# A decoder trunk in split fp32r products: inverse roots by one ScalarE function, LayerNorm sums by fp32r products, four more warm products, and the first sums moved into the third product group

## The chip, the core and the metric

The kernel runs on one core of a Trainium2 chip. The metric is device time in microseconds (us). The program is one launch over one step of a decoder trunk: 288 tokens (256 of a new sequence and 8 times 4 of running ones), width 2048, one layer, MLP width 8192.

## What is computed

```python
def trunk_layer(x, hist_conv, hist_pool, pos0, ...):
    h = rmsnorm(x, norm1_g)                              # x * rsqrt(mean(x*x) + EPS) * g
    proj = einsum("btd,de->bte", h, w_in) + b_in         # 2048 -> 1024 + 1024 + 1024
    a, gate, z = proj[..., :1024], proj[..., 1024:2048], proj[..., 2048:]
    u = a * sigmoid(gate)
    u_ext = concatenate([hist_conv, u], axis=1)          # 30 tokens of history
    c = silu(layernorm(depthwise_causal_conv(u_ext, conv_w, conv_b), ln_g, ln_b))   # 31 taps
    z_ext = concatenate([hist_pool, z], axis=1)          # 15 tokens of history
    d = multiscale_pool(z_ext, pos0)                     # windows 2, 4, 8, 16: mean - z
    p = einsum("btgc,gce->btge", d, pool_w) * pool_scale # four groups of 256
    x = x + einsum("btm,md->btd", concatenate([c, p]), w_out)
    f = square(relu(einsum("btd,df->btf", rmsnorm(x, norm2_g), w_ff1)))
    x = x + einsum("btf,fd->btd", f, w_ff2)
    return x, u_ext[:, -30:], z_ext[:, -15:]
# then y = rmsnorm(x, norm_f); both token sets share all weights
```

## The kernel before

Channels lie on the 128 partitions and the 288 tokens along the free axis. Every weight block and every activation is split into two fp32r parts, hi (a rounded copy) and lo (the rest), and each product of a 128x128 weight tile with 128x288 activations is three TensorE (PE) matmuls: hi by hi, lo by hi, hi by lo. All of them are recorded at line L305, in `mm`. The weights come once from memory by DMA on SP's queue into the tile `wr` (six buffers). The hi part `whi` is a cast on ScalarE (ACT), L274; the lo part `wlo` is a subtraction on VectorE (DVE), L279, or in two halves on GpSimd (POOL), L282, or a DMA that accumulates, L277. The string table `WAYS` says which block goes which way. Both parts have five buffers each, so a new cast has to wait until PE has read the block five before it.

The order of the program is: nine warm products (L213, L214) on a constant; sixteen blocks of `x` with their weights, split by `first_split` (L364 to L376); then one product group after another as the tuple `SEQUENCE` lists them: `c0` to `c7` are pairs of columns for the convolution branch (`c0` and `c1` run as one group of 384 products, `c2` is the second group, with 192), `p3` to `p0` are the input columns of the pool branch (`pool_group`), `P3` to `P0` its own small products (`pool_products`, tile `pp`). Then come eight product groups of `w_out` on the pool branch (right-hand side `dx`), eight on the convolution branch (`mx`), and four rounds of the MLP.

The first RMSNorm is not applied before the products but after them. `squares()` adds up x*x on ACT and DVE. `first_sums` (L524) sums over partitions by three small matmuls into PSUM tile `pt`, and `rsqrt_sums` turns the 96x3 sums into inverse roots: a DVE step (L249), a square root on ACT (L250), the load of the next ACT function table (L209), then four DVE steps (L253 to L256, one of them a reciprocal, one Newton step). `first_rows` (L528) spreads them over the partitions by three fp32 matmuls (`spread`), and ACT copies the result to the row `rb` (L530). A dictionary `between` says ahead of which pair of blocks of a group PE does this: the sums ahead of the last pair of the first group, the spread ahead of the second pair of `c2`. `conv_pair` and `pool_group` multiply their products by `rb` (L445, L483).

The convolution is 31 taps per pair of columns, each a DVE instruction of 128x256 (L461). `conv_pair` puts them under `later()`, a lower priority, so that the scheduler fills DVE with them between the steps that PE waits for. For the samples POOL makes all products at once (`prd`, L464) and DVE adds them (L466). In `pool_group` the scaled input `tz` (L483) becomes `z_all`; POOL adds windows (L492), mends the first columns (`rcnt`, L496), DVE makes the difference `d` (L497), POOL that of the samples (L499, L500), and `d` is split into `dx` hi (ACT, L502) and lo (DVE, L503). `pool_products` reads the product tile `pp` and writes `dx` again (L514, L515).

LayerNorm: `ln_mean` sums 1024 channels by two fp32 products with a matrix of ones (tile `pmean`); `ln_sums` centres, squares (L566) and adds (L570, L571) and calls `rsqrt_sums`; `ln_rows` spreads; the loop behind (L592 to L598) scales, applies Silu, and splits the result into `mx`. The second RMSNorm (`second_rows`) and the final one take the square root on ACT and call `inverse_root`, a DVE reciprocal (L233) and three more DVE steps. PSUM tiles made by `ms` (`warm`, `pt`, `pp`, `pmean`, `ends`) all use one single buffer.

Each engine runs its instructions in the order in which the scheduler put them, and an instruction that waits holds up all behind it on its engine.

Of the kernel before, what the change touches and what calls it, by code (L numbers as in the profile page):

```python
# [16 lines left out]
P = 128  # L17
D = 2048
# [68 lines left out]
def trunk_kernel(ctx: ExitStack, tc: tile.TileContext, io):  # L87
# [18 lines left out]
    def nm(s):  # L106
        seen[s] = seen.get(s, 0) + 1
        return f"{s}{seen[s]}"
# [25 lines left out]
    def f32(t):  # L134
        return t.bitcast(F32)
# [20 lines left out]
    def v(key, j):  # L156
        return vec[:, OFF[key] + j : OFF[key] + j + 1]
# [48 lines left out]

    def load_table(func, src):

        return nc.scalar.activation(few[: src.shape[0], :], src, func)  # L209

    load_table(AF.Sqrt, ones[:, 0:1])
    warm = ms("warm")
    for j in range(9):  # L213
        nc.tensor.matmul(warm[:, 0, 0:P], ones, ones, start=True, stop=True)  # L214
    ident = const.tile([TB, TB], F32, name="ident", padded_shape=[TB, TB + 40])
    make_identity(nc, ident)
# [9 lines left out]
    cst = const.tile([P, 32], F32, name="cst")  # L226
    eps, mean_d = cst[:, 0:1], cst[:, 1:2]
    nc.vector.memset(eps, EPS)
    nc.vector.memset(mean_d, 1.0 / D)

    def inverse_root(mean, root, y, out):

        nc.vector.reciprocal(y, root)  # L233
        nc.vector.scalar_tensor_tensor(out=root, in0=mean, scalar=EPS, in1=y, op0=ALU.add, op1=ALU.mult)
        nc.vector.scalar_tensor_tensor(out=root, in0=root, scalar=-0.5, in1=y, op0=ALU.mult, op1=ALU.mult)
        nc.vector.scalar_tensor_tensor(out=out, in0=root, scalar=1.5, in1=y, op0=ALU.add, op1=ALU.mult)

    def rsqrt_sums(parts, scale, after=None):

        pq = ms("pt")
        pt = pq[:, 0, :]
        for n, t in enumerate(parts):
            for j in range(3):
                last = mm(pt[:TB, j : j + 1], t[:, j * TB : (j + 1) * TB], ones[:, 0:1], start=n + j == 0, stop=n == len(parts) - 1 and j == 2)
        st = const.tile([TB, 12], F32, name=nm("st"))
        s = [st[:, 3 * j : 3 * j + 3] for j in range(4)]
        nc.vector.tensor_scalar(s[0], pt[:TB, 0:3], scale * DC, EPS, op0=ALU.mult, op1=ALU.add)  # L249
        nc.scalar.activation(s[1], s[0], AF.Sqrt)  # L250
# [3 lines left out]
        nc.vector.tensor_tensor(s[3], s[2], s[2], op=ALU.mult)  # L254
        nc.vector.scalar_tensor_tensor(out=s[3], in0=s[3], scalar=-0.5, in1=s[0], op0=ALU.mult, op1=ALU.mult)
        nc.vector.scalar_tensor_tensor(out=s[2], in0=s[3], scalar=1.5, in1=s[2], op0=ALU.add, op1=ALU.mult)  # L256
# [45 lines left out]
    def mm(*args, **kw):  # L302

        with tc.issue_after(chain[-1]) if chain else nullcontext():
            last = nc.tensor.matmul(*args, **kw)  # L305
        if chain:
            chain[0] = last.ins
        return last
# [50 lines left out]
    def first_split(k0):  # L359
        firsts.append([by_pair(t) for t in spl()])  # L360
        raw, hi, lo = raws[k0 // 2], *firsts[k0 // 2]
        blocks = [slice(i, i + 1) for i in range(2)] if k0 < 4 else [slice(0, 2)]
        hx.extend(halves(act2("hx")))
        nc.scalar.copy(hi[:, blocks[0]], raw[:, blocks[0]])  # L364
        for k in range(k0, k0 + 2):
            if k == 0:
                nc.vector.tensor_scalar(hx[k][0], xT[:, k, :], v("norm1_g", k), None, op0=ALU.mult)  # L367
            else:
                nc.scalar.activation(hx[k][0], xT[:, k, :], AF.Copy, scale=v("norm1_g", k))  # L369
        for b in blocks[1:]:  # L370
            nc.scalar.copy(hi[:, b], raw[:, b])
        for b in blocks:
            nc.vector.tensor_tensor(lo[:, b], raw[:, b], f32(hi[:, b]), op=ALU.subtract)
# [37 lines left out]
    def squares():  # L411

        nc.scalar.copy(scratch[:, :, :, 0:1], f32(firsts[2][0])[:, 1, 1, 0:10].rearrange("p (n k t) -> p n k t", n=5, t=1))
        for q in range(8):
            xq = xT[:, 2 * q : 2 * q + 2, :]
            a = q // 4
            dst = scratch[:, 2 + q % 3] if q % 4 else tot[a]
            nc.scalar.activation(dst, xq, AF.Square)
            if q % 4:
                nc.vector.tensor_tensor(tot[a], tot[a], dst, op=ALU.add)  # L420
        nc.vector.tensor_tensor(tot[0], tot[0], tot[1], op=ALU.add)
        nc.vector.tensor_tensor(tot[0][:, 0, :], tot[0][:, 0, :], tot[0][:, 1, :], op=ALU.add)
        return [tot[0][:, 0, :]]
# [98 lines left out]
    pair1 = [cvp.tile([P, 512], F32, name=nm("ac"), tag="cv") for m in range(2)]  # L522

    def first_sums():  # L524
        diag.append(rsqrt_sums(squares(), 1.0 / D, AF.Sigmoid))
        return diag[0][2]

    def first_rows():  # L528
# [10 lines left out]
    for kind, i in SEQUENCE[3:]:  # L539
# [5 lines left out]
            pool_group(i)  # L545
        else:
            pool_products(i)
    load_table(AF.Sqrt, f32(mixp[1][0])[:, 0:1])
# [4 lines left out]

    norm = {}

    def ln_mean():
        norm["mean"] = ms("pmean")[:, 0, :T]
        mm(norm["mean"], ones, sum_c[:, 0, :], start=True, stop=False)
        return mm(norm["mean"], ones, cs[-1][:, 1, :], start=False, stop=True)

    def ln_sums():
        ssc = None
        for c in cs:
            nc.vector.tensor_tensor(c, c, norm["mean"][:, None, :].to_broadcast([P, 2, T]), op=ALU.subtract)
            q = tmpp.tile([P, 2, T], F32, name=nm("q2"), tag="ag" if ssc is None else "ag2", bufs=2)
            nc.scalar.activation(q, c, AF.Square)  # L566
            if ssc is None:
                ssc = q
            else:
                nc.vector.tensor_tensor(ssc, ssc, q, op=ALU.add)  # L570
        nc.vector.tensor_tensor(ssc[:, 0, :], ssc[:, 0, :], ssc[:, 1, :], op=ALU.add)  # L571
        norm["sums"] = rsqrt_sums([ssc[:, 0, :]], 1.0 / DC, AF.Silu)
        return norm["sums"][2]

    def ln_rows():
        norm["rows"], last = spread(norm["sums"])
# [11 lines left out]

    mixc = []
    for j, c in enumerate(cs):  # L590
        n = tmpp.tile([P, 2, T], F32, name=nm("n"), tag="ag", bufs=2)
        nc.vector.tensor_tensor(n, c, norm["rows"][:, None, :].to_broadcast([P, 2, T]), op=ALU.mult)  # L592
        for m in range(2):
            i = 2 * j + m
            nc.scalar.activation(n[:, m, :], n[:, m, :], AF.Silu, bias=v("ln_b", i), scale=v("ln_g", i))  # L595
        mh, ml = act2("mx")
        nc.scalar.copy(mh, n)  # L597
        nc.vector.tensor_tensor(ml, n, f32(mh), op=ALU.subtract)  # L598
        mixc += halves((mh, ml))


# [36 lines left out]
    def second_rows():  # L638

        hl = actp.tile([P, 4, T], F32R, name="hl", tag="act")  # L640
        hi, lo = hl[:, 1, :], hl[:, 0, :]
        nc.scalar.copy(hi, ss2)
        nc.vector.tensor_tensor(lo, ss2, f32(hi), op=ALU.subtract)
        bk, r2 = ms("mean2"), row("r2")
        mean, root = bk[:, 0, :T], bk[:, 1, :T]
        mm(mean, means, hi, start=True, stop=False)
        last = mm(mean, means, lo, start=False, stop=True)
        nc.scalar.activation(root, mean, AF.Sqrt, bias=eps)
        inverse_root(mean, root, r2, r2)
        rows2.append(r2)  # L650
        return last

# [55 lines left out]
    nc.scalar.activation(root, sums_f, AF.Sqrt, bias=eps[:TB, :])  # L708
    inverse_root(sums_f, root, first, s_f)
    for spread_f in (rows_f, again):  # L710
        for j in range(3):
# [72 lines left out]
```

## Time and profile before

| what | value |
|---|---|
| time, median of three runs | 1084.62 us (1084.41 to 1085.51) |
| time of the profiled execution | 1084.57 us |
| its span, first to last instruction | 1082.8 us |
| PE busy | 1071.5 us (99%), 8198 matmuls |
| DVE busy | 635.4 us (59%), 818 instructions |
| ACT busy | 479.0 us (44%), 585 instructions |
| POOL busy | 173.6 us (16%), 180 instructions |
| mean granted TensorE clock | 0.997 |

The profile is of one execution, and times in it count from the first instruction. Between the span and the time of the same execution lie 1.8 us. An engine is called busy while an instruction of its own is under way, also when that instruction takes longer than its like elsewhere in the trace.

### The profile page before, as it was taken

To read this page: it belongs to the slowest core of one execution; us is meant where nothing else is said; L and a number is where in the kernel's file an instruction comes from. 1 tells how busy PE (TensorE), PEld (TensorE's weight loads), DVE (VectorE), ACT (ScalarE), POOL (GpSimd) and SP (SyncE) were. 2 spreads that over 40 slices of the span, in tenths; PEclk is the share of its full clock that TensorE was granted. 3 is DMA by queue.
4 is the path that set the end of the run, shared out by engine and by line. 5 is a ranking of instruction groups with operands and counts; after the bars stand their busy time and mean duration, and the time that the engine had idled before them with its cause. 6 is when DMAs were issued, how large, how long until landed. Compare 5 with 4: busy or idle time off the path is not lost.

```text
span 1082.8 us, 19572 instructions
## 1 busy us (share of the span) xinstructions
PE 1071.5 (99%) x8198; PEld 1069.9 (99%) x8198; DVE 635.4 (59%) x818; ACT 479.0 (44%) x585; POOL 173.6 (16%) x180
## 2 busy tenths in 40 slices
PE   9999999999999999999999999999999999999996
PEld 9999999999999999999999999999999999999996
DVE  8899999678655544445544444545544445554553
ACT  8654445475544433334443333444433334444441
POOL 0878979512000000000000000000000000000001
PEclk9999999999999999999999999999999999999998
DMA  9896468545555555555555555555555555555522
GB/s 325 281 273 185 137 196 239 176 152 177 173 164 170 172 166 169 174 164 169 171 168 168 175 165 169 174 167 167 174 165 168 174 169 165 173 166 168 173 78 88
DMA packets 58296, 190.71 MB, mean 176 GB/s; under 512 B 6240, under 2 KB 11232, under 8 KB 58208
## 3 DMA queue, kind: packets, MB, share of 16 engines
q1 hardware_dynamic: 56336, 184.35, 53.9%
q0 software_dynamic: 1008, 3.67, 1.9%
q8 instruction: 64, 1.05, 0.4%
q10 hardware_dynamic: 864, 1.44, 0.4%
q14 instruction: 24, 0.20, 0.1%
HBM read 185.16 MB, written 4.28 MB: 175 GB/s over the span
## 4 chain that ended last, share of the span: by engine, by line
PE 77%; issue 20%; ACT 1%; DVE 0%; DMA 0%; POOL 0%; POOLq 0%
PE ac L305 77%; PE pp L305 1%; DMA wr<-in_w 0%; ACT whi L274 0%; POOL xT L720 0%; ACT n L595 0%; DVE wlo L279 0%; PE pt L305 0%; PE pmean L305 0%; POOLq L770 0%; DVE xT L695 0%; DVE n L592 0%; ACT whi L364 0%; ACT mx L597 0%; DVE hx L367 0%
## 5 line engine op out<-in xcount | busy, mean ns | idle before, releaser
L274 ACT CAST whi<-wr 128x1024 fp32r<-128x1024 f32 (+1 forms) x332 | 348.0, 1049 | 551.4 <-PE ac L305 533.5
L279 DVE TENSOR_TENSOR wlo<-wr,whi 128x1024 fp32r<-128x1024 f32 x288 | 353.1, 1226 | 348.5 <-ACT whi L274 348.5
L305 PE MATMUL ac<-ax,whi 128*128 128x288 f32 x2048 | 351.0, 292 | 0.0
L305 PE MATMUL ac<-fx,whi 128*128 128x288 f32 x2048 | 350.2, 292 | 0.0
L305 PEld LDWEIGHTS ac<-ax,whi 128*128 128x128 f32 x2048 | 296.0, 187 | 0.0
L305 PEld LDWEIGHTS ac<-fx,whi 128*128 128x128 f32 x2048 | 295.6, 187 | 0.0
L305 PE MATMUL ac<-ax,wlo 128*128 128x288 f32 x1024 | 217.4, 292 | 0.0
L305 PE MATMUL ac<-fx,wlo 128*128 128x288 f32 x1024 | 216.4, 292 | 0.0
L305 PEld LDWEIGHTS ac<-ax,wlo 128*128 128x128 f32 x1024 | 162.6, 187 | 0.0
L305 PEld LDWEIGHTS ac<-fx,wlo 128*128 128x128 f32 x1024 | 162.3, 187 | 0.0
L305 PE MATMUL ac<-hx,whi 128*128 128x288 f32 x768 | 131.8, 295 | 1.2 <-DVE hx L367 1.2
L720 POOL TENSOR_TENSOR xT<-xT,rf 128x288 f32<-128x288 f32 x4 | 3.1, 795 | 800.1 <-ACT rf L724 800.1
L305 PEld LDWEIGHTS ac<-hx,whi 128*128 128x128 f32 x768 | 112.1, 190 | 1.4 <-ACT hx L369 1.4
L282 POOL TENSOR_TENSOR wlo<-wr,whi 128x512 fp32r<-128x512 f32 x74 | 100.3, 1410 | 35.3 <-ACT whi L274 34.3
L461 DVE SCALAR_TENSOR_TENSOR pc<-u_all,vec,pc 128x256 f32<-128x256 f32 x232 | 99.5, 483 | 1.9 <-ACT pc L458 0.7
L305 PE MATMUL ac<-hx,wlo 128*128 128x288 f32 x384 | 80.1, 294 | 0.0
L305 PEld LDWEIGHTS ac<-hx,wlo 128*128 128x128 f32 x384 | 61.1, 190 | 0.0
L305 PE MATMUL ac<-dx,whi 128*128 128x288 f32 x256 | 46.0, 296 | 0.0
L305 PE MATMUL ac<-mx,whi 128*128 128x288 f32 x256 | 45.1, 294 | 0.1
L664 DVE SCALAR_TENSOR_TENSOR t<-ac,r 128x576 f32<-128x576 f32 x32 | 24.2, 758 | 25.1 <-PE ac L305 25.1
L305 PEld LDWEIGHTS ac<-dx,whi 128*128 128x128 f32 x256 | 38.0, 188 | 0.2
L305 PEld LDWEIGHTS ac<-mx,whi 128*128 128x128 f32 x256 | 37.5, 188 | 0.6 <-ACT mx L597 0.4
(133 smaller groups left out, 533.6 us busy)
## 6 DMA issues: line engine op xcount, KB each, us to landing
wr<-in_w SPq DMA_DIRECT2D x335, 512.0 KB, 3.8
wlo<-in_w POOLq DMA_DIRECT2D x7, 512.0 KB, 7.7
xT<-in_xT SPq DMA_DIRECT2D x8, 288.0 KB, 7.3
wr<-in_w SPq DMA_DIRECT2D x5, 256.0 KB, 3.6
out_u_out<-u_all SPq DMA_DIRECT2D x1, 1208.0 KB, 9.3
u_all<-in_hist_c SPq DMA_DIRECT2D x8, 136.0 KB, 6.2
out_z_out<-z_all SPq DMA_DIRECT2D x1, 668.0 KB, 9.9
z_all<-in_hist_p SPq DMA_DIRECT2D x4, 152.0 KB, 7.5
```

Of the source, the lines that this page charges most:

```text
L274: nc.scalar.copy(hi, raw)
L279: nc.vector.tensor_tensor(lo, raw, f32(hi), op=ALU.subtract)
L282: nc.gpsimd.tensor_tensor(lo[:, j : j + 2, :], raw[:, j : j + 2, :], f32(hi[:, j : j + 2, :]), op=ALU.subtract)
L305: last = nc.tensor.matmul(*args, **kw)
L461: nc.vector.scalar_tensor_tensor(out=dst, in0=up[:, w : w + SEQ], scalar=cwv[:, w : w + 1], in1=pc, op0=ALU.mult, op1=ALU.add)
L664: nc.vector.scalar_tensor_tensor(out=t, in0=bk[:, :, :T], scalar=0.0, in1=both(rows2[0]), op0=ALU.max, op1=ALU.mult)
L720: eng.tensor_tensor(xk, xk, r[:, None, :].to_broadcast([P, n, T]), op=ALU.mult)
```

## The change

All square roots with reciprocals become one ACT function, `Abs_reciprocal_sqrt`, which adds EPS by its bias, and the Newton step behind it stays as three DVE steps. `rsqrt_sums` loses its first DVE step: the sums are made with a column of 1/D, and ACT reads them from PSUM. Nine warm products become thirteen. In `first_split` the first activation's scaling on DVE is put ahead of the first weight subtraction. `first_sums` moves out of the first group into `c2`, ahead of its second pair; the spread moves ahead of its third pair. LayerNorm's mean is made by four fp32r products of split parts (`hm`, `means_c`) and its sum of squares by two, directly on all partitions, so that `ln_rows` and its spread go; the inverse root is then taken of a 128x288 row. Several DVE additions of that part change their form, and the part is recorded under `later(-LATER)`, a higher priority.

```diff
-    def inverse_root(mean, root, y, out):
-        nc.vector.reciprocal(y, root)
-        ... three scalar_tensor_tensor
+    def inverse_root(mean, y, t, out, after=None):
+        nc.scalar.activation(y, mean, AF.Abs_reciprocal_sqrt, bias=eps[: y.shape[0], :])
+        if after is not None:
+            load_table(after, y[:, 0:1])
+        ... three scalar_tensor_tensor
...
-    for j in range(9):
+    for j in range(13):
         nc.tensor.matmul(warm[:, 0, 0:P], ones, ones, start=True, stop=True)
...
-        nc.vector.tensor_scalar(s[0], pt[:TB, 0:3], scale * DC, EPS, op0=ALU.mult, op1=ALU.add)
-        nc.scalar.activation(s[1], s[0], AF.Sqrt)
-        if after is not None:
-            load_table(after, s[1][:, 0:1])
-        nc.vector.reciprocal(s[2], s[1])
-        nc.vector.tensor_tensor(s[3], s[2], s[2], op=ALU.mult)
-        ... two scalar_tensor_tensor
+        inverse_root(pt, *s, after=after)
...
         for b in blocks:
-            nc.vector.tensor_tensor(lo[:, b], raw[:, b], f32(hi[:, b]), op=ALU.subtract)
+            with tc.issue_after(first.ins) if k0 == 0 else nullcontext():
+                nc.vector.tensor_tensor(lo[:, b], raw[:, b], f32(hi[:, b]), op=ALU.subtract)
...
-    chain.append(gemm(pair0 + pair1, hx, between={15: first_sums}, classes="01" * 18 + TURN, by_part=True))
-    third = conv_products(2, between={2: first_rows}, classes="01" * 9 + TURN)
+    chain.append(gemm(pair0 + pair1, hx, classes="01" * 18 + TURN, by_part=True))
+    third = conv_products(2, between={2: first_sums, 4: first_rows}, classes="01" * 15 + TURN)
...
+    def low_part(eng, lo, part, hi):
+        nc.scalar.copy(hi, part)
+        ... lo = part - hi on DVE (scalar_tensor_tensor) or POOL (tensor_tensor)
+    hm = actp.tile([P, 4, T], F32R, name="hm", tag="act")
+    low_part(nc.gpsimd, hm[:, 0, :], sum_c[:, 0, :], hm[:, 1, :])
+    low_part(nc.vector, hm[:, 2, :], cs[-1][:, 1, :], hm[:, 3, :])
...
     def ln_mean():
-        mm(norm["mean"], ones, sum_c[:, 0, :], start=True, stop=False)
-        return mm(norm["mean"], ones, cs[-1][:, 1, :], start=False, stop=True)
+        return products(norm["mean"], [hm[:, j, :] for j in (1, 0, 3, 2)])
     def ln_sums():
+        with later(-LATER):
...
-                nc.vector.tensor_tensor(ssc, ssc, q, op=ALU.add)
+                nc.vector.scalar_tensor_tensor(out=ssc, in0=ssc, scalar=1.0, in1=q, op0=ALU.mult, op1=ALU.add)
...
-        norm["sums"] = rsqrt_sums([ssc[:, 0, :]], 1.0 / DC, AF.Silu)
+            low_part(nc.vector, hs[:, 0, :], ssc[:, 0, :], hs[:, 1, :])
+            bk, rl = ms("pt"), row("rl")
+            last = products(bk[:, 0, :T], [hs[:, 1, :], hs[:, 0, :]])
+            norm["rows"] = bk[:, 1, :T]
+            inverse_root(bk[:, 0, :T], rl, norm["rows"], norm["rows"], after=AF.Silu)
-    BETWEEN = {5: {4: ln_mean}, 6: {6: ln_sums}, 7: {2: ln_rows}}
+    BETWEEN = {5: {4: ln_mean}, 6: {6: ln_sums}}
...
     for j, c in enumerate(cs):
+        with later(-LATER):
...
-        nc.scalar.activation(root, mean, AF.Sqrt, bias=eps)
-        inverse_root(mean, root, r2, r2)
+        inverse_root(mean, r2, root, r2)
...
-    nc.scalar.activation(root, sums_f, AF.Sqrt, bias=eps[:TB, :])
     inverse_root(sums_f, root, first, s_f)
```

Line numbers in the changed kernel are two to eighteen off: `whi` casts are L271, `wlo` L276 (DVE) and L279 (POOL), the ACT root L235, the Newton steps L238 to L240.

The engines' orders move in three places. The first is ACT around the root of the first sums. `st1` holds the roots, `few` is the output of the table load, `rb1` the spread row, and the numbers of `whi` count weight blocks; this is before:

```order
L274 CAST whi11_492<-wr11_488 128x1024
L250 ACTIVATE st1_459<-st1_459 96x3
L209 ACT_TABLE_LOAD
L209 ACTIVATE few_114<-st1_459 96x1
L274 CAST whi12_497<-wr12_490 128x1024
L274 CAST whi13_607<-wr13_603 128x1024
L530 COPY rb1_247<-pt1_455 128x288
```

And ACT at the same place in the changed kernel:

```order
L271 CAST whi11_469<-wr11_465 128x1024
L271 CAST whi12_474<-wr12_467 128x1024
L271 CAST whi13_611<-wr13_607 128x1024
L235 ACTIVATE st1_513<-pt1_509,cst_167 96x3
L209 ACT_TABLE_LOAD
L209 ACTIVATE few_114<-st1_513,ones_112 96x1
L271 CAST whi14_616<-wr14_609 128x1024
L528 COPY rb1_253<-pt1_509 128x288
```

Two weight casts that stood behind the root and its table load now stand ahead of the root.

The second is DVE at the pool group `p2` and the convolution pair `c6`: `s7`, `d2` and `dx2` belong to the pool group, `ac10` holds the products of `c6` that are gated into `u_all`, `pc3` and `pc4` are the running sums of taps. Before:

```order
L445 TENSOR_TENSOR ac10_1588<-ac10_1588,rb1_247 128x288
L279 TENSOR_TENSOR wlo42_1857<-wr42_1854,whi42_1856 128x512
L461 SCALAR_TENSOR_TENSOR pc3_1061<-u_all_87,vec_85,pc3_1061 128x256
L497 SCALAR_TENSOR_TENSOR d2_1535<-s7_1532,z_all_91 128x2x256
L449 SCALAR_TENSOR_TENSOR u_all_87<-ac10_1588,vec_85,tg7_1713 128x256
L449 SCALAR_TENSOR_TENSOR u_all_87<-ac10_1588,vec_85,tg7_1713 128x8x4
L461 SCALAR_TENSOR_TENSOR pc3_1061<-u_all_87,vec_85,pc3_1061 128x256 x3
L461 SCALAR_TENSOR_TENSOR pc4_1718<-u_all_87,vec_85,pc4_1718 128x256
L461 SCALAR_TENSOR_TENSOR pc3_1061<-u_all_87,vec_85,pc3_1061 128x256
L503 TENSOR_TENSOR dx2_1540<-d2_1535,dx2_1540 128x2x288
```

And DVE at the same place in the changed kernel:

```order
L495 SCALAR_TENSOR_TENSOR d2_1539<-s7_1536,z_all_91 128x2x256
L459 SCALAR_TENSOR_TENSOR pc3_1065<-u_all_87,vec_85,pc3_1065 128x256
L443 TENSOR_TENSOR ac10_1592<-ac10_1592,rb1_253 128x288
L459 SCALAR_TENSOR_TENSOR pc3_1065<-u_all_87,vec_85,pc3_1065 128x256
L276 TENSOR_TENSOR wlo42_1861<-wr42_1858,whi42_1860 128x512
L443 TENSOR_TENSOR ac10_1592<-ac10_1592,rb1_253 128x288
L459 SCALAR_TENSOR_TENSOR pc3_1065<-u_all_87,vec_85,pc3_1065 128x256 x2
L447 SCALAR_TENSOR_TENSOR u_all_87<-ac10_1592,vec_85,tg7_1717 128x256
L447 SCALAR_TENSOR_TENSOR u_all_87<-ac10_1592,vec_85,tg7_1717 128x8x4
L459 SCALAR_TENSOR_TENSOR pc3_1065<-u_all_87,vec_85,pc3_1065 128x256
L501 TENSOR_TENSOR dx2_1544<-d2_1539,dx2_1544 128x2x288
```

The difference `d2` now stands ahead of both gate products instead of behind them, and `dx2` has one tap between it and `u_all` instead of five; the set of steps up to the next pool group's `tz` is the same. On POOL the step of L496 that `d2` waits for now stands ahead of the two halves of weight block 41 instead of behind them.

The third is DVE at LayerNorm's sums: `q21` holds the squares, `st2` and `pt2` the roots, `n1` the scaled rows, `xT` the residual. Before:

```order
L571 TENSOR_TENSOR q21_2690<-q21_2690 128x288
L279 TENSOR_TENSOR wlo70_2805<-wr70_2798,whi70_2804 128x1024
L249 TENSOR_SCALAR st2_2709<-pt2_2705 96x3
L253 RECIPROCAL st2_2709<-st2_2709 96x3
L254 TENSOR_TENSOR st2_2709<-st2_2709 96x3
L255 SCALAR_TENSOR_TENSOR st2_2709<-st2_2709 96x3
L256 SCALAR_TENSOR_TENSOR st2_2709<-st2_2709 96x3
L587 TENSOR_TENSOR xT_86<-xT_86,ac20_2652 128x576
L279 TENSOR_TENSOR wlo71_2892<-wr71_2887,whi71_2891 128x1024
L592 TENSOR_TENSOR n1_2809<-c1_638,pt2_2705 128x576
```

And DVE at the same place in the changed kernel:

```order
L587 SCALAR_TENSOR_TENSOR q21_2701<-q21_2701 128x288
L276 TENSOR_TENSOR wlo70_2813<-wr70_2806,whi70_2812 128x1024
L558 SCALAR_TENSOR_TENSOR hs_2716<-q21_2701,hs_2716 128x288
L238 SCALAR_TENSOR_TENSOR pt2_2719<-pt2_2719,rl1_2720 128x288
L239 SCALAR_TENSOR_TENSOR pt2_2719<-pt2_2719,rl1_2720 128x288
L604 TENSOR_TENSOR xT_86<-xT_86,ac20_2663 128x576
L240 SCALAR_TENSOR_TENSOR pt2_2719<-pt2_2719,rl1_2720 128x288
L276 TENSOR_TENSOR wlo71_2900<-wr71_2895,whi71_2899 128x1024
L610 TENSOR_TENSOR n1_2817<-c1_642,pt2_2719 128x576
```

The lo part `hs` of the summed squares, which PE's two products read, stands behind the weight step `wlo70`. On ACT the root follows the cast of `hs` hi, and two weight casts (`whi71`, `whi72`) instead of one now stand between the table load and the first Silu.

More of the change, by code (lines that the diff above doesn't have):

```diff
@@ L547, in trunk_kernel @@
             pool_products(i)
[L548 removed]
+    load_table(AF.Abs_reciprocal_sqrt, f32(mixp[1][0])[:, 0:1])
     with later(2 * LATER):
@@ L556, in ln_mean, with products @@
+    def products(bank, parts):
+        for j, part in enumerate(parts):
+            last = mm(bank, means_c, part, start=j == 0, stop=j == len(parts) - 1)
+        return last
     def ln_mean():
         norm["mean"] = ms("pmean")[:, 0, :T]
-        mm(norm["mean"], ones, sum_c[:, 0, :], start=True, stop=False)
-        return mm(norm["mean"], ones, cs[-1][:, 1, :], start=False, stop=True)
+        return products(norm["mean"], [hm[:, j, :] for j in (1, 0, 3, 2)])
     def ln_sums():
-        ssc = None
@@ L590, in trunk_kernel @@
     for j, c in enumerate(cs):
[L591 to L598, printed above, removed]
+        with later(-LATER):
+            n = tmpp.tile([P, 2, T], F32, name=nm("n"), tag="ag", bufs=2)
+            nc.vector.tensor_tensor(n, c, norm["rows"][:, None, :].to_broadcast([P, 2, T]), op=ALU.mult)
+            for m in range(2):
+                i = 2 * j + m
+                nc.scalar.activation(n[:, m, :], n[:, m, :], AF.Silu, bias=v("ln_b", i), scale=v("ln_g", i))
+            mh, ml = act2("mx")
+            nc.scalar.copy(mh, n)
+            nc.vector.scalar_tensor_tensor(out=ml, in0=n, scalar=1.0, in1=f32(mh), op0=ALU.mult, op1=ALU.subtract)
         mixc += halves((mh, ml))
```

55 lines of the change are left out of this document (29 added, 26 removed).

## The prediction

> **What bounds the kernel now.** I read the page's busy shares first, then what PE waited for, then a table of stretches.
>
> ```profile
> PE 1071.5 (99%) x8198; PEld 1069.9 (99%) x8198; DVE 635.4 (59%) x818; ACT 479.0 (44%) x585; POOL 173.6 (16%) x180
> PE ac L305 <- DVE hx L367: 1.2, 1, 1.2
> PE warm L214 <- DVE cst L229: 1.0, 1, 1.0
> ```
>
> PE is busy for 1071.5 of 1082.8 us, and its two longest listed waits, 1.2 and 1.0 us, both lie at the start. So the kernel ends when PE has made its products. The change can gain only by fewer or faster steps on PE, or in the short chains where PE starts and stops; it can lose wherever a helper engine comes later than PE wants it. The table of stretches says where that is near. Its columns are the stretch, its length, then busy us and instructions of PE, its weight loads, DVE, ACT and POOL, then clock, DMA share and GB/s.
>
> ```profile
> 128.00:173.00 45.00, 45.00 (x345) 44.90 (x345) 44.89 (x93) 24.55 (x38) 35.05 (x33) 1.00 0.64 191
> ```
>
> From 128 to 173 us, in the pool groups, DVE has 0.11 us of idle time in 45. PE does not wait there, but DVE has no room left to catch up.
>
> **The start.** The timeline of the first microseconds:
>
> ```profile
> 1.04 4.21 PE L214 MATMUL warm<-ones 128*128 128x128 f32 x18 [1.04 <-DVE cst L229]
> 6.40 1.30 PE L305 MATMUL ac<-hx,whi 128*128 128x288 f32 x4 [1.15 <-DVE hx L367]
> 8.45 2.12 PE L305 MATMUL ac<-hx,whi 128*128 128x288 f32 x8
> 11.00 1.76 PE L305 MATMUL ac<-hx,whi 128*128 128x288 f32 x12
> 16.59 1.22 DVE L373 TENSOR_TENSOR wlo<-wr,whi 128x1024 fp32r<-128x1024 f32 x1
> 18.94 1.21 PE L305 MATMUL ac<-hx,wlo 128*128 128x288 f32 x8
> ```
>
> Nine warm products take 4.21 us, 0.47 each; thirteen end at about 7.1, where the real products now begin at 6.40. That costs 0.7. Against it, products up to about 10.4 are spaced 0.24 us apart (8.45 to 10.37 for eight) and later ones 0.13 (11.00 to 12.59 for twelve). Sixteen stand in the slow stretch; if they run at the later spacing, 16 times 0.11 is 1.8 us saved. PE cannot keep all of the difference: the weight step at 16.59 ends at 17.81, and PE uses such a block at 18.94, so PE can be early by 1.1 at most before it waits for DVE. The start gains 1.1, with 0 as the other end if the clock does not rise earlier. The hx step that now stands ahead of the weight step only serves the start that the warm products cover: nothing.
>
> **The first sums.** These decide whether the 1.1 is kept. The timeline of PE, ACT, DVE, SP's queue and POOL, and from the tile view of `wr` how long its loads of 24 to 40 us took to land:
>
> ```profile
> 32.47 0.59 PE L305 MATMUL pt<-ones,z_all 128*96 128x1 f32 x6
> 35.74 0.91 PE L305 MATMUL pt<-ident,st 96*128 96x96 f32 x6
> 29.48 1.06 ACT L274 CAST whi<-wr 128x1024 fp32r<-128x1024 f32 x1 [2.29 <-DMA wr<-in_w]
> 33.28 0.21 ACT L250 ACTIVATE st<-st 96x3 f32<-96x3 f32 x1 [1.44 <-DVE st L249]
> 25.25 1.30 SPq L169 DMA_DIRECT2D wr<-in_w  x2
> DMA to landing us min/median/max: 5.2/6.5/8.5
> 33.73 0.51 DVE L254 TENSOR_TENSOR st<-st 96x3 f32<-96x3 f32 x1
> 34.27 1.22 DVE L255 SCALAR_TENSOR_TENSOR st<-st 96x3 f32<-96x3 f32 x1
> 35.52 0.16 DVE L256 SCALAR_TENSOR_TENSOR st<-st 96x3 f32<-96x3 f32 x1
> 32.94 2.54 POOL L282 TENSOR_TENSOR wlo<-wr,whi 128x512 fp32r<-128x512 f32 x2
> ```
>
> The sums now stand 20 products later: 32.5 less 1.1 plus 20 times 0.13 is 34.0; they take 0.45, and 12 products on, at 36.0, PE wants the spread. Before, ACT had the root done at 33.5 because casts 12 and 13 stood behind it. Now it stands behind them, and casts here wait for their loads (the row at 29.48 waited 2.29 for one). The loads of blocks 12 and 13 are the two issued from 25.25 on, the second at about 25.9; at the median of the view it lands at 32.4, at the longest at 34.4. By the 29.48 row block 10 took over 5 us and later ones queue behind, so I take the long end: the cast of 1.06 ends at 35.5, the root of 0.21 at 35.7.
>
> Then come three DVE steps. In the rows they took 0.16 where nothing else ran and 0.51 and 1.22 while POOL's block of 32.94 to 35.48 ran; the long one ends with it, at 35.49. Such a small step with both inputs in SBUF waits, by this trace, for a POOL instruction under way. The Trainium skill's page "SBUF — State Buffer", section "Who interferes with whom", says that a DVE instruction with two SBUF inputs contends with a GpSimd instruction that reads SBUF, and that the shared ports are locked for the whole instruction of whichever came first. The trace agrees here: 1.22 against 0.16. By that rule alone, a half block of POOL's is the price of each such meeting.
>
> Unhindered, three steps 0.2 apart end at 36.3. POOL's next two halves, 1.27 each, can hold them for one half or most of both, so the roots come between 36.3 and 38.2 and the spread a tenth later, where PE wants it at 36.0. Before, the spread began at 35.74, 20 products behind the sums; with some 0.7 for itself and 12 more products at 0.13, PE stood at 38.0. Now it stands between 37.1 and 39.0 there: 0.9 earlier to 1.0 later. The early 1.1 is spent in the wait. Because the held step above ended only with POOL's second half, I take **+0.5**, for start and sums together.
>
> **The pool groups.** The order of DVE and POOL shifts here. DVE first, POOL second, then other rows:
>
> ```profile
> 121.14 3.10 DVE L461 SCALAR_TENSOR_TENSOR pc<-u_all,vec,pc 128x256 f32<-128x256 f32 x6
> 127.57 0.69 DVE L497 SCALAR_TENSOR_TENSOR d<-s,z_all 128x512 f32<-128x512 f32 x1 [0.96 <-POOL s L496]
> 130.95 0.98 DVE L503 TENSOR_TENSOR dx<-d,dx 128x576 fp32r<-128x576 f32 x1
> 135.73 1.21 DVE L279 TENSOR_TENSOR wlo<-wr,whi 128x1024 fp32r<-128x1024 f32 x1
> 151.92 1.33 DVE L497 SCALAR_TENSOR_TENSOR d<-s,z_all 128x512 f32<-128x512 f32 x1
> 124.37 2.98 POOL L282 TENSOR_TENSOR wlo<-wr,whi 128x512 fp32r<-128x512 f32 x2
> 129.12 2.19 POOL L464 TENSOR_TENSOR prd<-u_all,vec 128x992 f32<-128x992 f32 x1
> 137.92 2.55 POOL L282 TENSOR_TENSOR wlo<-wr,whi 128x512 fp32r<-128x512 f32 x2 [2.52 <-ACT whi L274]
> 150.18 2.53 POOL L282 TENSOR_TENSOR wlo<-wr,whi 128x512 fp32r<-128x512 f32 x2
> 167.44 0.50 DVE L515 SCALAR_TENSOR_TENSOR dx<-pp,vec,dx 128x288 fp32r<-128x288 f32 x1
> 168.44 0.43 PE L305 MATMUL pp<-dx,whi 128*128 128x288 f32 x2
> ```
>
> First, the difference L497 stood behind both gate products and waited 0.96 for POOL's L496. Now DVE is there four taps into the row at 121.14 (0.52 each), at 123.2. L496 now takes the place where POOL's pair began, 124.4 to 124.6. Behind it POOL goes straight on with that pair, whose first half lasts 1.5, and L497 reads two SBUF tiles: it took 0.69 with POOL free and 1.33 beside the pair at 150.18. If POOL gets in first, L497 starts at 126.0, 2.8 after DVE came, 1.8 more than before; if not, 1.4 after, 0.45 more. POOL needs no signal from another engine and DVE needs POOL's, so I take 1.8.
>
> Second, the lo step L503 stood five taps of about 0.5 behind `u_all`, just as POOL's `prd` of 2.19 us, started by the same `u_all`, was ending: it took 0.98. With one tap between, it comes 0.5 behind `u_all` and finds nearly all of `prd` before it: about 1.7 of wait, in place of some 0.2 of the 0.36 from its start at 130.95 to the end of `prd` at 131.31: 1.5; none if it gets in first. Third, with DVE 3.3 late the weight step of 135.73 moves to 139.0, into POOL's pair of 137.92 to 140.47, from which it was clear: up to one half, 1.0 taken.
>
> DVE is then 4.3 late (0.45 to 4.6). The nearest thing that PE waits for is the single buffer of `pp`: DVE's L515 frees it at 167.94 and PE takes it at 168.44, 0.5 of slack. The stretch has no idle time in DVE that could give it back, and DVE's work here starts from gates that come from PE, so the 0.5 of the first sums is in addition. PE loses 4.3 less 0.5: **+3.8**, 0 to 4.1.
>
> **LayerNorm.** The rows of PE, ACT and DVE:
>
> ```profile
> 201.31 0.97 PE pmean L305 x4
> 210.11 0.59 PE L305 MATMUL pt<-ones,q 128*96 128x1 f32 x6
> 213.82 0.80 PE L305 MATMUL pt<-ident,st 96*128 96x96 f32 x6
> 214.41 0.51 PE L305 MATMUL ac<-dx,whi 128*128 128x288 f32 x2
> 208.94 0.46 DVE L571 TENSOR_TENSOR q<-q 128x288 f32<-128x288 f32 x1
> 209.84 1.23 DVE L279 TENSOR_TENSOR wlo<-wr,whi 128x1024 fp32r<-128x1024 f32 x1 [0.44 <-ACT whi L274]
> 219.55 0.30 PEld L305 LDWEIGHTS ac<-mx,whi 128*128 128x128 f32 x2 [0.35 <-ACT mx L597]
> ```
>
> Savings on PE: the mean goes from 0.97 to four fp32r products of 0.13, 0.45 less; the sums from 0.45 to 0.26, 0.2 less; the spread goes, 214.41 less 213.82, 0.6. Together 1.2. New wait: the lo part of the summed squares stands on DVE behind `wlo70`, which ends at 211.07; a 128x288 step of 0.46 makes it 211.5, and PE wants it at 210.2: 1.3. Last, one more weight cast stands ahead of Silu. `mx` was already 0.35 late; a cast is 1.06 (the row at 29.48), some of it in time that ACT waits anyway; 0 to 1.1, I take 0.6. In sum **+0.7**, from -1.2 to +1.2. The second RMSNorm is nothing: neither of PE's two longest waits is there.
>
> **The tail.**
>
> ```profile
> 1071.57 0.17 DVE L233 RECIPROCAL cst<-cst 96x3 f32<-96x3 f32 x1 [1.53 <-ACT cst L708]
> 1071.85 0.16 DVE L234 SCALAR_TENSOR_TENSOR cst<-ends,cst 96x3 f32<-96x3 f32 x1
> ```
>
> The reciprocal goes from the last chain: 1071.85 less 1071.57, **-0.3**.
>
> **The sum.** 0.5 + 3.8 + 0.7 - 0.3 is +4.7. The profiled execution took 1084.57 us, 1.8 more than its span and 0.05 less than the median, and I let the 1.8 stand: 1089.3.
>
> **The rivals.** (1) DVE does not fall late: L497, L503 and the weight step get in before POOL, or the 0.5 of slack takes what is left. For it speaks that the same steps are done in the same stretch and that PE waits for none of them now; against it, that four of the long rows above (0.51, 1.22, 0.98, 1.33) lie beside POOL. Then 0.5 + 0.7 - 0.3: +0.9, 1085.5. (2) Faster: the same, and besides the two loads ahead of the root come in time, so that the spread is there at 36.0 and the 1.1 of the start is kept, and `hs` finds DVE free, so that the 1.2 of LayerNorm is kept: -1.1 - 1.2 - 0.3 is -2.6, 1082.0. It decides at the root: with ACT done with cast 13 by 34.2, and no POOL block over the Newton steps, the wait is gone. The 2.29 that ACT waits for a load at 29.48 speaks against it. (3) More meetings with POOL than I count, as each late step moves the next: high ends, 1.0 + 4.1 + 1.2 - 0.3 is +6.0, 1090.6, and a further half block of 1.27 makes it 1091.8.
>
> **How the numbers follow.** My forecast gets 0.61, rival 1 0.20, rival 2 0.13, rival 3 beyond the range 0.06. The forecast's own ends are 1086 and 1090.6. To leave out no more than two in ten the range goes down past rival 1 and stops short of rival 2: 1084.0 to 1091.6. A measurement of this kernel tells about 0.2%, 2.2 us, from no change. Faster than that is most of rival 2, also where it goes a little better: 0.13. Rival 1 and the forecast's low end lie within it: 0.22. The rest is slower: 0.65.
>
> **What would show it.** In the changed profile: warm products to about 7.1 and spacing of 0.13 right behind; a PE wait at the spread for `st`; a root that starts behind the cast of block 13; L495 waiting over 2 us for POOL and L501 over 1.5 us long; a wait of PE at a `pp` product near 168, of 3 to 4 us; a PE wait of about 1.3 for `hs`; 0.3 less between the last sums and the last spread. I am wrong if PE shows no wait between 40 and 173, or if the spread is not waited for.

## The result and the profile after

The changed kernel takes 1094.53 us (median of four runs, 1094.11 to 1094.98), the kernel before 1085.03 us in the same comparison: 1.0091 of its time, with a 95% interval of 1.0076 to 1.0106, or 9.5 us slower. The forecast was 4.7 us slower, and the time lies above the range. The profiled execution has a span of 1092.5 us where before it was 1082.8: 9.7 us.

The page of the changed kernel, its busy shares, and then what PE waited for:

```profile
PE 1073.6 (98%) x8196; PEld 1071.0 (98%) x8196; DVE 646.1 (59%) x814; ACT 478.9 (44%) x588; POOL 175.0 (16%) x182
PE pmean L302 <- DVE hm L558: 4.7, 1, 4.7
PE pt L302 <- DVE st L240: 1.5, 1, 1.5
PE warm L214 <- DVE cst L231: 1.0, 1, 1.0
PE pt L302 <- DVE hs L558: 0.9, 1, 0.9
PE ac L302 <- ACT mx L615: 0.6, 1, 0.6
PE ac L302 <- DVE wlo L276: 0.6, 1, 0.6
PE pp L302 <- ACT dx L500: 0.4, 1, 0.4
```

The waits for `st`, `hs` and `mx` are among those that the prediction named; the 0.4 us at `pp` is for ACT's `dx` and not for the buffer of `pp`. The longest, 4.7 us at LayerNorm's mean, was not in it. The timeline of DVE, ACT, POOL and PE there:

```profile
198.35 0.48 DVE L459 SCALAR_TENSOR_TENSOR c<-u_all,vec,pc 128x256 f32<-128x256 f32 x1
198.86 0.43 ACT L556 CAST hm<-c 128x288 fp32r<-128x288 f32 x1
199.33 9.59 DVE L558 SCALAR_TENSOR_TENSOR hm<-c,hm 128x288 fp32r<-128x288 f32 x1 [0.50 <-ACT hm L556]
195.42 5.03 POOL L279 TENSOR_TENSOR wlo<-wr,whi 128x512 fp32r<-128x512 f32 x4
200.41 0.80 POOL L560 TENSOR_TENSOR hm<-sum_c,hm 128x288 fp32r<-128x288 f32 x1
201.18 7.42 POOL L279 TENSOR_TENSOR wlo<-wr,whi 128x512 fp32r<-128x512 f32 x6
203.69 0.55 PE L302 MATMUL pmean<-hm,means_c 128*128 128x288 f32 x3
208.97 0.61 PE L302 MATMUL pmean<-hm,means_c 128*128 128x288 f32 x1 [4.73 <-DVE hm L558]
210.34 1.16 PE L302 MATMUL ac<-dx,whi 128*128 128x288 f32 x4
214.41 0.70 PE L302 MATMUL ac<-dx,whi 128*128 128x288 f32 x4
220.34 0.45 DVE L558 SCALAR_TENSOR_TENSOR hs<-q,hs 128x288 fp32r<-128x288 f32 x1
```

The last tap ends at 198.8, and ACT has the hi part at 199.3, over 4 us before PE wants it. Then DVE's lo step, which takes 0.45 where it is alone (`hs`, the same form, in the last line), shows 9.59 us. POOL runs a row of eleven instructions without a gap, from 195.42 to 208.60; the last eight lie beside DVE's step, which ends 0.3 us behind them. And when PE goes on, its products are spaced 0.24 us apart (the row at 210.34) and only near 214 again 0.13: the pause is followed by some 20 products at half pace, 2.3 us more. The granted clock stands at 0.5 from 207.3 to 214.1 us.

PE's lag against before, read at the same products of the two profiled executions, adds up to the result:

| place | before, us | after, us | lag, us |
|---|---|---|---|
| first product behind the spread (same count) | 38.0 | 38.63 | +0.6 |
| last pool product `pp` | 168.44 | 171.05 | +2.6 |
| first product of the mean | 201.31 | 203.69 | +2.4 |
| products for the sum of squares | 210.11 | 219.55 | +9.4 |
| first `mx` product | 219.55 | 229.86 | +10.3 |
| last sums (`ends`) | 1069.38 | 1079.39 | +10.0 |
| last spread | 1072.45 | 1082.17 | +9.7 |

### The profile page after: what moved, and what is told of

Read it like the earlier page. It is cut to its first block, busy times and chain, and to the rows that moved or that the text cites. A ratio compares the mean times of both kernels' runs of the same rounds, so it can differ in the third digit from the quotient of the medians.

```text
span 1092.5 us, 19567 instructions
## 1 busy us (share of the span) xinstructions
PE 1073.6 (98%) x8196; PEld 1071.0 (98%) x8196; DVE 646.1 (59%) x814; ACT 478.9 (44%) x588; POOL 175.0 (16%) x182
## 4 chain that ended last, share of the span: by engine, by line
PE 66%; issue 21%; DVE 6%; POOL 3%; DMA 2%; ACT 1%; SPq 0%; POOLq 0%; ACTq 0%
PE ac L302 65%; DVE pc L459 2%; DMA wr<-in_w 2%; POOL s L490 1%; POOL wlo L279 1%; DVE hm L558 1%; DVE wlo L276 1%; DVE dx L501 0%; ACT whi L271 0%; DVE d L495 0%; DMA u_all<-in_hist_c 0%; POOL xT L736 0%; DVE c L464 0%; PE pp L302 0%; DVE dx L513 0%
## 5 line engine op out<-in xcount | busy, mean ns | idle before, releaser
L271 ACT CAST whi<-wr 128x1024 fp32r<-128x1024 f32 (+1 forms) x332 | 346.7, 1045 | 548.0 <-PE ac L302 530.2
L276 DVE TENSOR_TENSOR wlo<-wr,whi 128x1024 fp32r<-128x1024 f32 x288 | 354.3, 1230 | 349.6 <-ACT whi L271 349.6
L279 POOL TENSOR_TENSOR wlo<-wr,whi 128x512 fp32r<-128x512 f32 x74 | 99.9, 1379 | 34.6 <-ACT whi L271 33.9
L302 PEld LDWEIGHTS ac<-dx,whi 128*128 128x128 f32 x256 | 39.5, 196 | 0.0
```

Of the source, the lines that this page charges most:

```text
L271: nc.scalar.copy(hi, raw)
L276: nc.vector.tensor_tensor(lo, raw, f32(hi), op=ALU.subtract)
L279: nc.gpsimd.tensor_tensor(lo[:, j : j + 2, :], raw[:, j : j + 2, :], f32(hi[:, j : j + 2, :]), op=ALU.subtract)
```

## Experiments

Theory L (lock-out): a DVE step with two inputs in SBUF does not get in as long as POOL's instructions follow one another without a gap, so it waits not for half a block but for the row. Theory D: DVE is late as a whole by the new order, and PE's wait at the mean is the end of that. Beside them stands the question whether the slow products are the clock's answer to PE's pause. All times are medians; the kernel before took 1084.7, 1084.9 and 1084.6 us in the three comparisons.

**The mean without split parts.**

```diff
-    hm = ... low_part(nc.gpsimd, ...); low_part(nc.vector, ...)
-        return products(norm["mean"], [hm[:, j, :] for j in (1, 0, 3, 2)])
+        mm(norm["mean"], ones, sum_c[:, 0, :], start=True, stop=False)
+        return mm(norm["mean"], ones, cs[-1][:, 1, :], start=False, stop=True)
```

> The changed kernel with the mean made by two fp32 products, as before, and without the split parts hm. Theory L (lock-out): VectorE's lo step of hm was held for 9.6 us by GpSimd's unbroken row of weight blocks, PE waited 4.7 us for it and then ran some 20 products at half pace, another 2.3 us, and both go while the mean costs 0.45 us more: 1094.5 - 4.7 - 2.3 + 0.4 = 1087.9 us. Theory D (VectorE is late as a whole, and PE would wait for the last tap all the same): the wait stays in good part, at least 1092 us.

Measured: 1087.74 us (ratio 1.0027, 1.0016 to 1.0038). The whole of wait and slow pace goes, as L expected; the last tap alone was not late. PE's timeline shows the mean with no wait and full pace behind it:

```profile
203.36 0.65 PE L302 MATMUL pmean<-sum_c,ones 128*128 128x288 f32 x2
203.85 0.65 PE L302 MATMUL pmean<-c,ones 128*128 128x288 f32 x2
204.12 0.65 PE L302 MATMUL ac<-dx,whi 128*128 128x288 f32 x2
204.60 0.43 PE L302 MATMUL ac<-dx,wlo 128*128 128x288 f32 x2
```

**Work for PE during the wait.**

```diff
+        for j in range(16):
+            ... nc.tensor.matmul(pm[:, 1, 0:P], ones, ones, start=True, stop=True)   # ahead of the fourth product
```

> The changed kernel with 16 products on a constant between the third and the fourth product of the mean, in a bank that nothing reads, so that PE works during about 4 us of its wait. If the slow pace after the wait is the clock answering to PE's pause, the wait stays but the 2.3 us behind it go: 1092.2 us, and the spacing after the mean is 0.13 us. If the slow pace has another cause (transfers, or GpSimd and VectorE catching up), the time stays at 1094.5 us.

Measured: 1093.18 us (1.0078, 1.0063 to 1.0093), between the two, and its interval meets that of the changed kernel. The trace settles it: DVE's step is as late as before, but the products behind the mean keep 0.13 us, and the granted clock does not fall there.

```profile
206.14 3.73 PE L579 MATMUL pmean<-ones 128*128 128x128 f32 x32
211.08 0.40 PE L302 MATMUL pmean<-hm,means_c 128*128 128x288 f32 x1 [1.21 <-DVE hm L558]
211.85 0.70 PE L302 MATMUL ac<-dx,whi 128*128 128x288 f32 x4
```

So the slow pace belongs to the pause. In this execution PE came to the mean at 205.75, 2 us later than in the changed kernel's, because the clock had fallen once already: PE waited 1.7 us for `st` at the first sums, and the granted clock was 0.5 from 39.5 to 42.9 us. This execution took 1094.20 us; the two shortest of the four runs, 1092.26 and 1092.54, lie where the clock's answer had put them. The Trainium skill's page "TensorE: Matmul & The Clock Gate", section "What's actually happening", says that the clock is halved by default and after an idle window of about 3.4 us, and full after a busy one, with windows that run freely. The changed kernel's trace agrees for its pause: 4.7 us idle, then 4.8 us at half pace. It does not agree everywhere: the 1.7 us above, and 1.6 us in an experiment below, were followed by half pace too, and there the measurement decides.

**The first sums back in place.**

```diff
-    chain.append(gemm(pair0 + pair1, hx, classes="01" * 18 + TURN, by_part=True))
-    third = conv_products(2, between={2: first_sums, 4: first_rows}, classes="01" * 15 + TURN)
+    chain.append(gemm(pair0 + pair1, hx, between={15: first_sums}, classes="01" * 18 + TURN, by_part=True))
+    third = conv_products(2, between={2: first_rows}, classes="01" * 9 + TURN)
```

> The changed kernel with the first sums and the spread back in their places of before; VectorE's order from the gates to the mean is then that of before, but for the one step of hm. Theory L: the pool groups' delay of 2.6 us goes, but VectorE's hm step meets GpSimd's row all the same and PE still waits 3 to 5 us with the slow pace behind: about 1091 to 1092.5 us. Theory D: the wait for hm goes with the delay, 1085 us or less.

Measured: 1089.16 us (1.0039, 1.0027 to 1.0051), less than L gave, with single runs from 1085.62 to 1091.40. The profiled one took 1091.40. With DVE 2.4 us earlier than in the changed kernel the step is kept out all the same, for 8.73 us, and PE waits 3.9:

```profile
196.95 8.73 DVE L558 SCALAR_TENSOR_TENSOR hm<-c,hm 128x288 fp32r<-128x288 f32 x1 [0.50 <-ACT hm L556]
197.91 7.45 POOL L279 TENSOR_TENSOR wlo<-wr,whi 128x512 fp32r<-128x512 f32 x6
205.74 0.61 PE L302 MATMUL pmean<-hm,means_c 128*128 128x288 f32 x1 [3.87 <-DVE hm L558]
```

Theory D falls: without the delay the wait is there, in this execution. The mean granted clock says something of the others: it is 0.997 or 0.998 in the four runs from 1085.62 to 1087.17 us, as it nearly always is in the kernel before, and 0.993 to 0.996 in the six from 1089.09 us on. So the short runs lack most of the slow pace. They must lack part of the wait as well, by this estimate: this kernel with the fp32 mean takes 1084.9 us (below), and 3.9 of wait less the 0.45 that the faster mean saves would make it 1088.3 without any slow pace. The same kernel was profiled once more:

> The changed kernel with the first sums back in place, once more, for a second profile of the same program: its ten runs lay between 1085.6 and 1091.4 us. If VectorE's hm step sometimes finds a gap in GpSimd's row, a run near 1086 us shows a short hm step and no slow products behind the mean, and one near 1091 us a step of 8 to 9 us as in the first profile.

It took 1090.46 us, again with the long step (8.75 us) and the wait of 3.9 us. No trace shows a run near 1086 us, so whether the step got in earlier there is open.

**A pause made in POOL's row.** One small POOL instruction that needs DVE's result stands behind the first pair of half blocks; every other order is that of the changed kernel.

```diff
+    touch = const.tile([P, 1], F32, name="touch")
+    nc.gpsimd.tensor_scalar(touch, f32(hm[:, 2, 0:1]), 1.0, None, op0=ALU.mult)
```

> The changed kernel with one added GpSimd instruction, a 128x1 copy out of VectorE's hm lo part, two half blocks behind GpSimd's own hm step: GpSimd has to pause there until VectorE's step is done; all else stands as it did. Theory L (a row of GpSimd instructions without a gap keeps VectorE's two-input step out): the pause lets it in at once, the step ends near 204 us, PE waits under 1 us and keeps its pace: 1094.5 - 4.4 - 2.3 = 1088 us. If VectorE's step was long for another reason (its own operands, PE's reads), the added wait only makes GpSimd later: 1094.5 us or more.

Measured: 1088.40 us (1.0034, 1.0021 to 1.0047). An instruction more, and a wait more, make the kernel 6 us faster. DVE, POOL and PE, which does not wait for the mean:

```profile
199.11 4.68 DVE L558 SCALAR_TENSOR_TENSOR hm<-c,hm 128x288 fp32r<-128x288 f32 x1 [0.50 <-ACT hm L556]
200.92 2.56 POOL L279 TENSOR_TENSOR wlo<-wr,whi 128x512 fp32r<-128x512 f32 x2
203.88 0.22 POOL L567 TENSOR_SCALAR touch<-hm 128x1 f32<-128x1 f32 x1 [0.40 <-DVE hm L558]
203.48 0.77 PE L302 MATMUL pmean<-hm,means_c 128*128 128x288 f32 x4
```

POOL's pair ends at 203.48, POOL stops for 0.40 us, and in that gap DVE's step ends, at 203.79. It had been kept out by four POOL instructions in a row until then. So POOL's row is what kept this step out, shown by one added instruction that leaves the order of the others in place.

As a rule for every such step, theory L goes too far. In the same execution DVE's first two additions of squares stood beside POOL's next row:

```profile
207.04 1.46 DVE L589 SCALAR_TENSOR_TENSOR q<-q,q 128x576 f32<-128x576 f32 x1
209.09 1.19 DVE L589 SCALAR_TENSOR_TENSOR q<-q,q 128x576 f32<-128x576 f32 x1
204.07 5.58 POOL L279 TENSOR_TENSOR wlo<-wr,whi 128x512 fp32r<-128x512 f32 x4
213.09 0.40 PE L302 MATMUL pt<-hs,means_c 128*128 128x288 f32 x1 [0.86 <-ACT hs L556]
214.13 0.40 PE L302 MATMUL pt<-hs,means_c 128*128 128x288 f32 x1 [0.64 <-DVE hs L558]
```

The first addition ended at 208.50, 1.15 us before the row did, at 209.65: it waited for POOL instructions too (0.75 is what it takes alone), but came in between two that follow without a gap. Why one step comes in there and another is kept out for the whole row, no run here shows. The two late additions also made `hs` late. PE waited twice for it, and the granted clock was 0.5 from 214.7 to 218.1 us, so this execution (1089.13 us) still holds a slow stretch.

**Both lo parts on POOL.**

```diff
-    low_part(nc.vector, hm[:, 2, :], cs[-1][:, 1, :], hm[:, 3, :])
+    low_part(nc.gpsimd, hm[:, 2, :], cs[-1][:, 1, :], hm[:, 3, :])
```

> The changed kernel with both lo parts of hm on GpSimd, so that no VectorE step stands beside the row. Theory L: the part comes in GpSimd's own order, one pair of half blocks behind the other, near 204.5 us; PE waits about 1 us and keeps its pace: 1088 us. If the last taps were simply too late for a mean at this place, the wait stays above 3 us: 1092 us or more.

Measured: 1090.77 us (1.0052, 1.0038 to 1.0065), not 1088. The wait at the mean is 0.27 us, as L had it. What was not foreseen is that POOL's row then goes on beside the squares: DVE's first addition takes 2.48 us in place of 0.75, `hs` is late, and the pause it makes halves the pace again. Here the addition ended only behind POOL's row, at 209.51, where in the kernel with the pause it came in before the end.

```profile
207.03 2.48 DVE L586 SCALAR_TENSOR_TENSOR q<-q,q 128x576 f32<-128x576 f32 x1
213.65 0.40 PE L302 MATMUL pt<-hs,means_c 128*128 128x288 f32 x1 [1.34 <-ACT hs L556]
214.69 0.40 PE L302 MATMUL pt<-hs,means_c 128*128 128x288 f32 x1 [0.64 <-DVE hs L558]
215.59 1.16 PE L302 MATMUL ac<-dx,whi 128*128 128x288 f32 x4
```

**The first sums moved alone.** The kernel before with only the two `between` lines of the change.

> The kernel before with only the first sums moved into the second group. If the new order of VectorE and GpSimd in the pool groups comes from this move alone and costs what the changed kernel shows at the last pool product (2.6 us), the time is 1085.0 + 2.6 = 1087.6 us. If the move costs only its own wait for the roots, about 0.6 us: 1085.6 us.

Measured: 1089.49 us (1.0043, 1.0026 to 1.006), 2 us more than the expectation. The order in the pool groups does come from this move, with the same long steps (1.75 and 2.60 us), and the roots are waited for 1.6 us. The rest is the clock again:

```profile
38.89 0.91 PE L305 MATMUL pt<-ident,st 96*128 96x96 f32 x6 [1.60 <-DVE st L256]
40.13 0.68 PE L305 MATMUL ac<-hx,wlo 128*128 128x288 f32 x2
43.84 0.43 PE L305 MATMUL ac<-hx,whi 128*128 128x288 f32 x2
```

Here 1.6 us of waiting were enough for half pace from 39.6 to 43.0 (14 products, 1.5 us), where the changed kernel waited 1.5 us at the same place and kept its pace.

**Gaps for DVE in the pool group.** On the first of these kernels (the mean without split parts), two small POOL instructions that read DVE's `d` and `dx` lo stand ahead of weight blocks 41 and 43.

```diff
+            hand[0] = nc.gpsimd.tensor_scalar(touch[:, 0:1], d[:, 0, 0:1], ...)            # ahead of block 41
+            hand[1] = nc.gpsimd.tensor_scalar(touch[:, 1:2], f32(dl[:, 0, 0:1]), ...)      # ahead of block 43 and prd
```

> The changed kernel with the mean by two fp32 products (as the first experiment, 1087.7 us) and two added GpSimd instructions of 128x1 that read VectorE's d and VectorE's dx lo part of the second pool group, ahead of weight block 41 and ahead of block 43 and prd, so that GpSimd pauses until VectorE's two steps are done. VectorE's order is the same but for two taps that move ahead of dx. If the lag of the pool groups comes from these two steps being kept out (1.76 and 2.59 us long in the changed kernel, 0.7 alone), they shorten to about 0.7 each, VectorE is 2 to 3 us earlier, PE's lag at the last pool product falls from 2.6 to 0.7 or less: 1085.6 to 1086.2 us. If the lag comes from the order itself or from the late start, 1087.7 us.

Measured: 1086.20 us (1.0015, 1.0006 to 1.0024), 1.3 us (0.0012) less than without them. The two intervals overlap, the single runs hardly do: 1085.07 to 1086.74 us with the gaps, 1086.69 to 1088.74 without. In the kernel of the first experiment, the steps were these:

```profile
125.14 1.76 DVE L495 SCALAR_TENSOR_TENSOR d<-s,z_all 128x512 f32<-128x512 f32 x1 [1.15 <-POOL s L494]
130.80 2.59 DVE L501 TENSOR_TENSOR dx<-d,dx 128x576 fp32r<-128x576 f32 x1
170.72 0.53 PE L302 MATMUL pp<-dx,whi 128*128 128x288 f32 x2
```

And with the gaps:

```profile
125.01 0.69 DVE L500 SCALAR_TENSOR_TENSOR d<-s,z_all 128x512 f32<-128x512 f32 x1 [1.14 <-POOL s L499]
131.36 0.75 DVE L508 TENSOR_TENSOR dx<-d,dx 128x576 fp32r<-128x576 f32 x1
169.40 0.53 PE L306 MATMUL pp<-dx,whi 128*128 128x288 f32 x2
```

Both are down to what they take alone, and PE has its last pool product 1.3 us earlier.

**The rest of the change.** First the kernel before with the roots by one function, thirteen warm products and the first scaling ahead:

> The kernel before with the roots by one ScalarE function, thirteen warm products and the first scaling ahead, but the first sums and LayerNorm as they were. VectorE's order from the gates to the mean is that of before. By the changed kernel's trace the start gives 0.4 to 1.1 us, of which the wait for the roots may take part, and the tail 0.3: 1085.0 - 0.7 to 1085.0 - 1.4, so 1083.6 to 1084.3 us. If the early start is lost in the wait for the roots, 1084.7 us.

Measured: 1084.64 us against 1084.91 (0.9999, 0.9990 to 1.0007), no difference that can be told. Its profiled span, 1081.9 us, is 0.9 less than that of before, but the runs do not bear that out. Then the changed kernel with first sums and mean as before:

> The changed kernel without the two parts found costly: first sums in place, mean by two fp32 products. What is left is the roots, thirteen warm products and LayerNorm's sum of squares on all partitions. Against the kernel before: PE's wait for the lo part of the squares 0.9, mx 0.3 later, spread -0.6, sums -0.2, tail and start as in the last experiment: 1084.9 + 0.4 = 1085.3 us, within 0.5.

Measured: 1084.88 us (1.0000, 0.9991 to 1.0009). So the two parts taken back are the whole loss, within about 1 us. Last, the same with the sum of squares by one fp32 product:

```diff
-            last = products(bk[:, 0, :T], [hs[:, 1, :], hs[:, 0, :]])
+            last = mm(bk[:, 0, :T], ones, ssc[:, 0, :], start=True, stop=True)
```

> The same with the sum of squares by one fp32 product on all partitions, so that no split part stands between. PE's 0.9 us wait for the lo part goes, the product costs 0.2 more, mx should be ready about 0.5 earlier: 1084.9 - 0.4 = 1084.5 us; a version that beats both kernels if the start's gain shows, else the same as before.

Measured: 1083.20 us against 1084.63 (0.9989, 0.9980 to 0.9998). This one beats both kernels, the one before by about 1.2 us, with an interval that ends just short of no change. It is 1.3 us less than was expected, and no run says why. PE needs no split part and does not wait for the sum:

```profile
209.08 0.65 PE L302 MATMUL pt<-q,ones 128*128 128x288 f32 x2
209.35 0.64 PE L302 MATMUL ac<-dx,whi 128*128 128x288 f32 x2
```

## Why the prediction was wrong

- **The start and the first sums** were right in mechanism. Thirteen warm products brought the faster pace at once, PE was early, and the root behind casts 12 and 13 with two Newton steps kept out by POOL (1.00 and 1.19 us) spent it: +0.6 where +0.5 was said, with a PE wait of 1.5 us for `st`. That the two agree so well is in part luck. At the product that stands at 45.06 us before, the lag is +0.7 here; it is -0.2 to +0.3 in four other executions whose program is the same up to there, and +2.7 in the one with work during the wait, where the clock answered to a wait of 1.7 us. That price was not in it. (By the trace, the first group has 192 PE instructions and `c2` 96, half of what the description of the kernel says; the 20 and 12 products of the prediction are right.)
- **The pool groups** were right in mechanism and too dear. L495 waited and ran 1.3 us longer than before (1.8 said), L501 1.6 (1.5 said), the weight step 1.46 in place of 1.21 us (1.0 said for that), PE's lag grew by 2.0 in place of 3.8. It grew in four steps of 0.3 to 0.8 us between 161 and 171 us, with listed waits of 0.4 us for ACT's `dx` and 0.6 for a weight block, and not in one wait of 3 to 4 us for the buffer of `pp`. The gaps made for DVE show that the two steps cost 1.3 us of the time.
- **LayerNorm** is the step that failed. The term "the mean goes from 0.97 to four fp32r products of 0.13, 0.45 less" priced PE's products alone. It left out the new DVE step that makes their operand, and so the wait of 4.7 us and the 2.3 us of slow clock behind it. The parts that were listed came near: `hs` made PE wait 0.9 (1.3 said), and from the sum of squares to `mx` the lag grew by 0.9, where 1.3 - 0.2 - 0.6 + 0.6 gives 1.1.
- **The price of a meeting** would have hidden the step even if it had been listed. The prediction took half a block of POOL's for each, by the rows at 33 and 152 us and by the rule of the Trainium skill's page "SBUF — State Buffer", section "Who interferes with whom", which is one whole instruction. In the changed kernel's pool group the trace agrees:

```profile
125.49 1.76 DVE L495 SCALAR_TENSOR_TENSOR d<-s,z_all 128x512 f32<-128x512 f32 x1 [1.16 <-POOL s L494]
125.41 3.00 POOL L279 TENSOR_TENSOR wlo<-wr,whi 128x512 fp32r<-128x512 f32 x2
150.85 2.54 POOL L279 TENSOR_TENSOR wlo<-wr,whi 128x512 fp32r<-128x512 f32 x2
```

  The step ended at 127.25, 1.16 us before POOL's pair, and the pair took 3.00 us in place of 2.54: DVE came in between its halves. By that price the `hm` step would end near 201 us (an estimate: the POOL instruction under way at 199.33 ends with its row of four at 200.45, and the step takes 0.45), over 3 us before PE wants it at 204.2, and no wait would follow. The runs showed 9.59 us: kept out by eight of POOL's instructions in the changed kernel, and by four, until the first gap, with the pause in POOL's row.
- **The tail** was right: 0.3 less between the last sums and the last spread.

Rival 3, more meetings with POOL than were counted, was the right kind, with a chance of 0.06; it put one further half block where a whole row stood.

What stays open is what lets a DVE step in between two POOL instructions in one place and not in another, and, perhaps by the same cause, why the kernel with the first sums back has runs 5 us apart.

## What to carry to other kernels

Ask of every new step on VectorE whether both inputs lie in SBUF and what GpSimd does just then: the price is at least what is left of one GpSimd instruction, it can be the whole row where they follow without a gap, and one GpSimd instruction that depends on the step can end it. A faster product is no gain where its operand has to be made first; price the operand's chain, not only the product. A wait of PE in the middle of the program costs more than its length where the clock falls behind it: here it was some 2 us more for a wait of several.

## What the hardware showed that was not expected

A VectorE instruction with two SBUF inputs was held for 9.59 us by eight GpSimd instructions without a gap; where a gap of 0.40 us was made, it ended there. Other such instructions came in between two GpSimd instructions that follow without a gap, and the second of these then took about 0.5 us longer.

The granted clock, where it fell in the middle of a program, stood at 0.5 for 3.4 or 6.8 us. It did so for 6.8 us with PE's waits of 4.7 us (changed kernel) and 3.9 us (first sums back), and for 3.4 us with the same 3.9 us in the second profile of that program. It also did so, for 3.4 us, with waits of 1.6 and 1.7 us for `st` and with two short waits close together (1.34 and 0.64 us, 0.86 and 0.64 us). The changed kernel's wait of 1.5 us for `st`, and the waits of 0.9 us for `hs` alone, left it at 1.
